# Seven-for-eight block products over three quarters of a feed-forward's depth, remainders by accumulating DMAs, and a down projection in two passes

## The chip, the cores and the metric

One core of a Trainium2 chip runs one launch of the kernel. The metric is the device time of that launch in microseconds (us), as the median of several runs. The engines that appear below are TensorE (PE; its weight loads are shown apart as PEld), VectorE (DVE), ScalarE (ACT), GpSimd (POOL) and SyncE (SP). SP and POOL are used here mainly as queues that issue DMAs; ACT issues a few.

## The reference, cut to what matters

The reference is one layer of a diffusion backbone over 256 latent tokens and 256 context tokens of width 2048: a half-step feed-forward, a mixing of tokens (attention and a long convolution), and a second half-step feed-forward. The change is in the first feed-forward, which runs over both streams:

```
def swiglu(h, w_up, w_down):
    gate, up = jnp.split(h @ w_up, 2, axis=-1)
    return (jax.nn.silu(gate) * up) @ w_down

def half_ffn(s, m, slot, g, w_up, w_down):
    h = modulate(rms_norm(s, g), chunk(m, 3 * slot), chunk(m, 3 * slot + 1))
    return s + 0.5 * chunk(m, 3 * slot + 2) * swiglu(h, w_up, w_down)
```

`w_up` is 2048 x 11264, `w_down` is 5632 x 2048, all in fp32. The vectors `m` (shift, scale, gate) come from a linear map of the conditioning, called adaLN below: nine chunks of 2048, of which two are made at the start and seven while the first feed-forward runs.

## The kernel before, in words

**Precision.** Each fp32 operand is split into a rounded part (hi) and a remainder (lo = value - hi), and a product is three matmuls: hi x hi, hi x lo and lo x hi (`mm3`, L238 to L241). For a weight, ACT makes hi by a copy and DVE makes lo by a subtraction (`weight`, L221 to L235, and `split_to`, L207 to L210).

**Up.** The hidden width is cut into 44 tiles j of 128 gate and 128 up columns. Tiles 0 to 2 (WAVE) are done first, together with the making of the normed input; tiles 3 to 43 run in the loop at the end of the first feed-forward, one after another, through `up` (L425). The input has 16 k-tiles of 128 rows; each is a pair of buffers (hi, lo) of 128 x (2 streams x 256 tokens). A tile j takes four pieces kq of four k-tiles each, and each piece is one weight load of 512 KB (128 x 1024) from SP's queue.

A plain piece is eight products (gate or up, times four k-tiles) with 512 columns, so 24 matmuls 512 wide. A block-product piece treats two k-tiles by (gate, up) and two streams as a 2 x 2 by 2 x 2 block matrix product and does it with seven products of half the width in place of eight (a Strassen-Winograd scheme): for two pairs of k-tiles, 14 products with 256 columns, so 42 matmuls 256 wide. It needs sums of activations, made once by `combine` (L377) for each pair of k-tiles on DVE and ACT; sums of weights, made for each piece on DVE in place (L405 to L407); and a final combination of four banks in `up` (L444 to L450). `prepare` (L397) makes the weights of a piece in two halves, of three and of four blocks of 128 columns; `products` (L412) lists its products. `QUADS = {3: 4, 2: 5}` says that piece 3 is a block product from tile 4 on and piece 2 from tile 5 on. Pieces 0 and 1 are plain in all tiles. The sums are made at the head of tiles 4 and 5, in one go.

The result of a tile goes through SiLU and a product, is split by `keep` (L455) into hi (ACT) and lo (DVE), and both go to DRAM (`act`) by POOL's queue, 256 KB each.

**Down.** `w_down` is cut into 11 groups g of four hidden tiles and eight pairs dq of two output tiles; a step (`step`, L470) is one weight load of 512 KB and 24 matmuls 512 wide. `down` (L486) runs passes: three output pairs, three, then two, and in each pass all 11 groups. For each group `fetch` (L460) brings four tiles x (hi, lo) back from DRAM, eight DMAs of 256 KB on POOL's queue, up to three uses ahead; at most ROOM = 5 groups are held, so a pass can begin with those that the pass before ended with. In the middle of a pass the residual input is loaded. The last APART = 3 groups of the last pass are done by stream, context first and then latent, in matmuls 256 wide, so that the norm of the context can be made beside the latent half (`NORM_PLAN` says how much of it behind each output tile).

**adaLN.** 224 blocks of 512 KB are loaded on SP's queue, each behind the last weight load, and reduced on DVE (L145), once or, for chunks that both streams use, twice. `hook` is called behind each piece of `up` and ahead of each step of `down`; `ada_hook` then does as many blocks as `ADA_RATES` says for one call (2.0 in tiles 4 and 5, then 0.7, and 1.27 in down).

**Order.** A planner places the instructions of each engine: it takes them in program order where their inputs and buffers are ready in its own model of time. Once placed, each engine and each DMA queue works strictly in order. Buffers are shared by tag: "u" has 58 of 2 KB a partition (activations, sums, fetched tiles, temporaries), "raw" four and "whi" and "wlo" three each for weights. PSUM has eight banks, in two tags "pa" and "pb" of four; tile j uses one tag, tile j + 1 the other.

## Time and profile before

| | |
|---|---|
| time, median of 3 runs | 2681.13 us (2680.35 to 2682.34) |
| the profiled execution's own time | 2687.43 us |
| its span on the core | 2685.6 us |
| mean granted clock of TensorE | 0.989 |
| up, tiles 3 to 43 | about 158 to 1038 us |
| down | about 1038 to 1567 us |
| busy in the span: PE, DVE, ACT, POOL | 2625.9, 1897.1, 1018.8, 165.5 us |
| DMA moved | 586.29 MB, mean 218 GB/s |

The profile is of one execution. "Busy" of an engine is the union of its instructions' times; matmuls overlap in the records, so a busy PE may still be slowed. A wait is put down to the instruction that released it last. "PEclk" is the clock granted to TensorE as a share of the full one. Line numbers (L241) are those of the kernel's text above.

### The profile page before, as it was taken

The numbers are of one execution on the slowest core, as the hardware profiler recorded it, in microseconds if no ns is written. First come the engines' busy times: TensorE is split into PE (matmuls) and PEld (weight loads), VectorE is DVE, ScalarE is ACT, GpSimd is POOL, SyncE is SP. The second block draws the span as 40 slices with busy tenths as digits, with TensorE's granted clock in tenths as the row PEclk, the third lists the DMA queues.
The fourth block names the chain that finished last, engine by engine and source line by source line (L and its number), as shares of the span: only waits on it lengthen the run. The fifth ranks groups of instructions, "written<-read, shape, count | busy, mean of one in ns | idle before, by whom it ended". The sixth has DMA issues, their size and how long they took to land.

```text
span 2685.6 us, 36384 instructions
## 1 busy us (share of the span) xinstructions
PE 2625.9 (98%) x13856; PEld 2219.3 (83%) x13856; DVE 1897.1 (71%) x2985; ACT 1018.8 (38%) x1339; POOL 165.5 (6%) x316
## 2 busy tenths in 40 slices
PE   8999999999999998999999999999999999999999
PEld 5677999999999996778777888888888888888887
DVE  5788878877787876678778497789765555554444
ACT  5343333333333332112112265457454444444333
POOL 1100000000000002410101100000000000000000
PEclk8999999999999998999999999999999999999999
DMA  9975555555555559987978855435545655556664
GB/s 357 359 264 182 202 204 196 197 184 193 205 203 192 191 190 330 393 288 242 306 256 276 288 172 184 145 110 160 201 157 190 190 190 189 189 189 206 201 202 158
DMA packets 182476, 586.29 MB, mean 218 GB/s; under 512 B 21020, under 2 KB 24029, under 8 KB 177949
## 3 DMA queue, kind: packets, MB, share of 16 engines
q1 hardware_dynamic: 139580, 500.20, 54.7%
q0 software_dynamic: 41952, 80.50, 9.7%
q10 hardware_dynamic: 768, 3.28, 0.3%
q8 instruction: 108, 1.77, 0.3%
q14 instruction: 68, 0.55, 0.1%
HBM read 556.61 MB, written 27.28 MB: 217 GB/s over the span
## 4 chain that ended last, share of the span: by engine, by line
PE 77%; DMA 10%; DVE 9%; issue 3%; ACT 1%; SPq 0%; DVEq 0%; ACTq 0%
PE pa L1216 10%; PE pa L1217 10%; PE pa L1215 10%; DMA adaw<-in_w_adaT_dram 8%; PE pb L241 6%; PE pa L239 6%; PE pb L239 6%; PE pa L240 6%; PE pb L240 6%; PE pa L241 6%; PE pa L247 3%; DVE adas L145 3%; DVE wlo L232 2%; PE pa L249 2%; PE pb L182 1%
## 5 line engine op out<-in xcount | busy, mean ns | idle before, releaser
L232 DVE TENSOR_TENSOR wlo<-raw,whi 128x1024 fp32r<-128x1024 f32 x558 | 681.5, 1223 | 436.4 <-ACT whi L228 434.8
L228 ACT CAST whi<-raw 128x1024 fp32r<-128x1024 f32 x558 | 586.6, 1052 | 953.8 <-PE pa L1217 413.4
L241 PE MATMUL pa<-u,wlo 128*128 128x512 f32 (+1 forms) x1338 | 461.9, 345 | 6.5 <-DVE wlo L232 6.4
L239 PE MATMUL pa<-u,whi 128*128 128x512 f32 (+1 forms) x1338 | 463.8, 347 | 4.3 <-DMA u<-act 2.2
L240 PE MATMUL pa<-u,whi 128*128 128x512 f32 (+1 forms) x1338 | 462.2, 346 | 5.1 <-DMA u<-act 4.7
L241 PE MATMUL pb<-u,wlo 128*128 128x512 f32 (+1 forms) x1296 | 445.4, 344 | 18.4 <-DVE wlo L232 9.6
L239 PE MATMUL pb<-u,whi 128*128 128x512 f32 (+1 forms) x1296 | 445.3, 344 | 4.4 <-ACT whi L208 3.5
L240 PE MATMUL pb<-u,whi 128*128 128x512 f32 (+1 forms) x1296 | 443.7, 343 | 1.2 <-DVE u L209 1.2
L1215 PE MATMUL pa<-whi,u 128*128 128x512 f32 x1060 | 413.9, 391 | 0.0
L1216 PE MATMUL pa<-wlo,u 128*128 128x512 f32 x1060 | 412.8, 390 | 0.2 <-DVE wlo L232 0.2
L1217 PE MATMUL pa<-whi,u 128*128 128x512 f32 x1060 | 412.8, 390 | 0.0
L241 PEld LDWEIGHTS pb<-u,wlo 128*128 128x128 f32 x1296 | 249.0, 193 | 51.2 <-DVE wlo L232 18.6
L239 PEld LDWEIGHTS pa<-u,whi 128*128 128x128 f32 x1338 | 255.4, 191 | 41.5 <-issue 4.5
L241 PEld LDWEIGHTS pa<-u,wlo 128*128 128x128 f32 x1338 | 255.7, 191 | 38.4 <-DVE wlo L232 8.5
L240 PEld LDWEIGHTS pa<-u,whi 128*128 128x128 f32 x1338 | 255.5, 191 | 36.7 <-DMA u<-act 6.4
L239 PEld LDWEIGHTS pb<-u,whi 128*128 128x128 f32 x1296 | 248.7, 192 | 33.8 <-ACT whi L208 3.9
L240 PEld LDWEIGHTS pb<-u,whi 128*128 128x128 f32 x1296 | 248.9, 192 | 29.2 <-DVE u L209 1.5
L145 DVE CUSTOM_DVE_ANT_0 adas<-adaw,crow,mod 128x1024 bf16<-128x1024 f32 x160 | 205.3, 1283 | 68.1 <-DMA adaw<-in_w_adaT_dram 65.5
L145 DVE CUSTOM_DVE_ANT_0 adas<-adaw,crow,cond 128x1024 bf16<-128x1024 f32 x160 | 205.1, 1282 | 58.4 <-DMA adaw<-in_w_adaT_dram 56.4
L208 ACT CAST whi<-raw 128x768 fp32r<-128x768 f32 (+1 forms) x158 | 148.8, 943 | 245.3 <-DVE raw L407 169.7
L209 DVE TENSOR_TENSOR wlo<-raw,whi 128x768 fp32r<-128x768 f32 (+1 forms) x158 | 171.7, 1089 | 89.8 <-ACT whi L208 87.3
L1216 PEld LDWEIGHTS pa<-wlo,u 128*128 128x128 f32 x1060 | 199.1, 188 | 41.5 <-DVE wlo L232 0.6
(326 smaller groups left out, 2817.0 us busy)
## 6 DMA issues: line engine op xcount, KB each, us to landing
adaw<-in_w_adaT_dram SPq DMA_DIRECT2D x222, 512.0 KB, 5.8
raw<-in_w_dn_dram SPq DMA_DIRECT2D x182, 512.0 KB, 4.3
raw<-in_w_up_dram SPq DMA_DIRECT2D x176, 512.0 KB, 3.5
raw<-in_w_up1q_dram SPq DMA_DIRECT2D x164, 512.0 KB, 3.9
u<-act POOLq DMA_DIRECT2D x184, 256.0 KB, 8.0
wrow<-in_w_ada_dram SPq DMA_DIRECT2D x32, 1024.0 KB, 9.1
act<-u POOLq DMA_DIRECT2D x88, 256.0 KB, 2.3
raw<-in_w_hy_dram SPq DMA_DIRECT2D x32, 512.0 KB, 3.5
```

Of the source, the lines that this page charges most:

```text
L145: V.tensor_tensor_reduce(out=sc, in0=t, in1=crow[i][:, b * (D // 2) : (b + 1) * (D // 2)], scale=1.0, scalar=mcol if b else bada[:, n : n ...
L208: S.copy(hi, src)
L209: V.tensor_sub(lo, src, hi.bitcast(F32))
L228: S.copy(hi, raw)
L232: V.tensor_sub(lo, raw, hi.bitcast(F32))
L239: PE.matmul(ps, w[0], xx[0], start=start, stop=False)
L240: PE.matmul(ps, w[0], xx[1], start=False, stop=False)
L241: return PE.matmul(ps, w[1], xx[0], start=False, stop=stop)
L247: PE.matmul(ps, w[0], x, start=start, stop=stop)
L1215: PE.matmul(ps[t], hi, w[0], start=start, stop=False)
L1216: PE.matmul(ps[t], hi, w[1], start=False, stop=False)
L1217: last = PE.matmul(ps[t], lo, w[0], start=False, stop=stop)
```

## The change

It has four parts.

1. Block products for three of the four pieces: piece 3 from tile 5, piece 2 from tile 7, piece 1 from tile 9. `combine` becomes a generator of four parts for each pair of k-tiles; one part is run by the hook behind each piece, from tile 3 on, and one sum, which overwrites part of a plain operand, is put in place at the end of the tile before its first use (`install`).
2. Piece 0 stays plain, but its weights are made without DVE: ACT writes hi and then -hi, and a DMA on POOL's queue adds the raw weights to it in SBUF, 256 KB for each of two halves. Its buffers come from "u".
3. `keep` does the same for the activation's remainder, in DRAM: hi and -hi are stored, then the value is added by a third DMA to what the second has stored.
4. Down runs in two passes of four output pairs, eight banks each; the last two groups (APART = 2) are done by stream, with two output tiles to a bank. The adaLN rates become 0.79 for each piece of up from tile 4 on and 1.25 for each step of down.

```diff
 WAVE = 3
 ADA_UP = (5, 7, 6, 8)
 ADA_DOWN = (2, 3, 4)
-ADA_RATES = (2.0, 0.7, 1.27)
-QUADS = {3: 4, 2: 5}
+ADA_RATES = (0.79, 1.25)
+QUADS = {3: 5, 2: 7, 1: 9}
 GT = JT // GRP
-PASSES = ((0, 1, 2), (3, 4, 5), (6, 7))
-ORDERS = ((9, 8, 10, 7, 6, 5, 4, 3, 2, 1, 0), tuple(range(GT)), tuple(reversed(range(GT))))
+PASSES = ((0, 1, 2, 3), (4, 5, 6, 7))
+ORDERS = ((9, 8, 10, 7, 6, 5, 4, 3, 2, 1, 0), tuple(range(GT)))
 ROOM = 5
-APART = 3
-NORM_PLAN = (0, 1, 0, 1, 0, 1, 1, 1, 1, 1, 1, 1)
+APART = 2
+NORM_PLAN = (0, 1, 0, 1, 0, 1, 1, 1, 1, 1, 1, 1, 1, 1, 1, 1)
 
 AWAKE = (17, 5)
 
...
             self.h = [None] * KT
             self.mm = mm3
             self.held = {}
-            self.sums = {}
+            self.sums, self.first = {}, {}
             self.wupq = a["w_up1q"]
 
         def open(self, alt=False):
...
             return mm
 
         def close(self, j, ps2):
-            sg = tmp2((P, 2, L))
+            sg = U((P, 2, L))
             S.activation(sg, ps2[0], AF.Silu)
             V.tensor_mul(sg, ps2[1], sg)
             self.keep(j, sg)
...
         def combine(self, kp):
 
             (h0, l0), (h1, l1) = self.h[2 * kp], self.h[2 * kp + 1]
-            a0, a1, b0, b1 = tmp((P, 2, L)), tmp((P, 2, L)), tmp2((P, 2, L)), tmp2((P, 2, L))
+            a0, a1, b0, b1 = (U((P, 2, L)) for _ in range(4))
             V.tensor_add(a0, h0.bitcast(F32), l0.bitcast(F32))
             V.tensor_add(a1, h1.bitcast(F32), l1.bitcast(F32))
+            yield
             V.tensor_add(b0[:, 0, :], a0[:, 1, :], a1[:, 1, :])
             V.tensor_sub(b1[:, 0, :], b0[:, 0, :], a0[:, 0, :])
+            yield
             V.tensor_sub(b1[:, 1, :], a0[:, 1, :], a0[:, 0, :])
             V.tensor_sub(b0[:, 1, :], a1[:, 0, :], b1[:, 0, :])
+            yield
             s23, s4 = split(b1, (P, 2, L)), U((P, 2, L), F32R)
-            split_to(b0[:, 0, :], h0[:, 1, :], l0[:, 1, :])
             split_to(b0[:, 1, :], s4[:, 0, :], s4[:, 1, :])
             self.sums[kp] = [(h0[:, 0, :], l0[:, 0, :]), (h1[:, 0, :], l1[:, 0, :]), (s4[:, 0, :], s4[:, 1, :]),
                              (h1[:, 1, :], l1[:, 1, :]), (h0[:, 1, :], l0[:, 1, :]),
                              tuple(t[:, 0, :] for t in s23), tuple(t[:, 1, :] for t in s23)]
+            self.first[kp] = b0[:, 0, :]
+            yield
+
+        def build(self):
+            for kq in QUADS:
+                for kp in (2 * kq, 2 * kq + 1):
+                    yield from self.combine(kp)
+
+        def install(self, kq):
+            for kp in (2 * kq, 2 * kq + 1):
+                split_to(self.first.pop(kp), *self.sums[kp][4])
 
         def quads(self, j, kq):
             return j >= QUADS.get(kq, JT)
 
         def prepare(self, j, kq):
 
-            if not self.quads(j, kq):
-                return [weight(self.wupq[j - WAVE, kq], (P, 2, 4, P))]
             raw = weight_load(self.wupq[j - WAVE, kq], (P, 2, 4, P))
             out = []
+            if kq == 0:
+                hi, lo = ([U((P, 4, P), F32R) for _ in range(2)] for _ in range(2))
+                for q in range(2):
+                    S.copy(hi[q], raw[:, q])
+                    S.activation(lo[q], hi[q].bitcast(F32), AF.Copy, scale=-1.0)
+                    nc.gpsimd.dma_start(lo[q], raw[:, q].bitcast(F32R), accum_op=ALU.add)
+                return [(hi, lo)]
+            if not self.quads(j, kq):
+                return [weight(None, (P, 2, 4, P), raw=raw)]
             for n in (3, 4):
                 if n == 4:
                     V.tensor_sub(raw[:, :, 0:4:3], raw[:, :, 3:4].broadcast_to((P, 2, 2, P)), raw[:, :, 0:3:2])
...
                     ps = banks[bank] if part is None else banks[bank][:, part, :]
                     xx = self.h[x] if part is None else self.sums[x[0]][x[1]]
                     left[bank] -= 1
-                    mm3(ps, [t[:, q, block] for t in w[n]], xx, left[bank] == total[bank] - 1, left[bank] == 0)
+                    mm3(ps, [t[q][:, block] if kq == 0 else t[:, q, block] for t in w[n]], xx, left[bank] == total[bank] - 1, left[bank] == 0)
                 w = None
                 if j == JT - 1 and kq == 1:
                     self.fetch(ORDERS[0][0])
                 self.hook()
+            for kq in QUADS:
+                if QUADS[kq] == j + 1:
+                    self.install(kq)
             if not total[2]:
                 return self.close(j, banks)
-            g, v, u = tmp((P, 2, L)), tmp2((P, 2, L)), T(up, (P, L), "mt", bufs=3)
+            g, v, u = tmp((P, 2, L)), U((P, 2, L)), T(up, (P, L), "mt", bufs=3)
             S.copy(g[:, 0, :], banks[2][:, 0, :])
             V.tensor_add(u, g[:, 0, :], banks[2][:, 1, :])
             V.tensor_add(g[:, 1, :], u, banks[3][:, 0, :])
...
             self.keep(j, v)
 
         def keep(self, j, act):
-            act = split(act, (P, 2, L))
-            for s_ in range(2):
-                nc.gpsimd.dma_start(actd[j][:, s_], act[s_])
+
+            hi, minus = U((P, 2, L), F32R), U((P, 2, L), F32R)
+            S.copy(hi, act)
+            S.activation(minus, hi.bitcast(F32), AF.Copy, scale=-1.0)
+            nc.gpsimd.dma_start(actd[j][:, 0], hi)
+            nc.gpsimd.dma_start(actd[j][:, 1], minus)
+            nc.gpsimd.dma_start(actd[j][:, 1], act.bitcast(F32R), accum_op=ALU.add)
 
         def fetch(self, g):
 
...
                         nc.gpsimd.dma_start(act[s_], actd[j][:, s_])
                     self.held[g].append(act)
 
-        def step(self, g, dq, banks, begin, end, parts=None, done_=None):
+        def step(self, g, dq, banks, begin, end, part=None, done_=None):
 
             whi, wlo = weight(self.wdown[g, dq], (P, GRP, 2, P))
             for i2 in range(2):
                 d = dq * 2 + i2
                 for jj, act in enumerate(self.held[g]):
-                    ps = banks[d]
-                    act = act if parts is None else [t[:, parts, :] for t in act]
-                    self.mm(ps, (whi[:, jj, i2, :], wlo[:, jj, i2, :]), act, begin and jj == 0, end and jj == GRP - 1)
-                if end:
-                    for i in range(2) if parts is None else (parts,):
-                        V.scalar_tensor_tensor(xd(i, d), ps[:, i, :] if parts is None else ps, mod[i][self.cm + 2][:, d : d + 1], xd(i, d),
-                                               op0=ALU.mult, op1=ALU.add)
+                    ps = banks[d] if part is None else banks[dq][:, i2, :]
+                    act = act if part is None else [t[:, part, :] for t in act]
+                    self.mm(ps, (whi[:, jj, i2, :], wlo[:, jj, i2, :]), act, begin and jj == 0 and not (i2 and part is not None),
+                            end and jj == GRP - 1 and (i2 == 1 or part is None))
+                if end and part is None:
+                    for i in range(2):
+                        self.add(i, d, ps[:, i, :])
                 if done_:
                     done_()
+            if end and part is not None:
+                for i2 in range(2):
+                    self.add(part, dq * 2 + i2, banks[dq][:, i2, :])
+
+        def add(self, i, d, ps):
+            V.scalar_tensor_tensor(xd(i, d), ps, mod[i][self.cm + 2][:, d : d + 1], xd(i, d), op0=ALU.mult, op1=ALU.add)
 
         def down(self, after):
 
             uses = [(p, g) for p in range(len(PASSES)) for g in ORDERS[p]]
             for n, (p, g) in enumerate(uses):
                 if g == ORDERS[p][0]:
-                    tags = (PA, PA, PA, PA, PB, PB) if p == 0 else (PB, PB, PA, PA, PA, PA) if p == 1 else (PB,) * 4
-                    banks = {2 * dq + i2: tags[2 * k + i2]((P, 2, L)) for k, dq in enumerate(PASSES[p]) for i2 in range(2)}
+                    banks = {2 * dq + i2: (PA, PB)[k // 2]((P, 2, L)) for k, dq in enumerate(PASSES[p]) for i2 in range(2)}
                 for _, soon in uses[n : n + 3]:
                     self.fetch(soon)
                     while len(self.held) > ROOM:
...
             yield
             rest = [g for _, g in uses[-APART:]]
             for part in (1, 0):
-                banks = {d: (PA if part else PB)((P, L)) for d in range(2 * PASSES[-1][0], KT)}
+                banks = {dq: (PA if part else PB)((P, 2, L)) for dq in PASSES[-1]}
                 for g in rest:
                     self.fetch(g)
                     for dq in PASSES[-1]:
...
     crow = []
 
     xs = [[None] * (KT // 2) for _ in range(2)]
-    ready = {j: kq for kq, j in QUADS.items()}
+    build = f1.build()
+    f1.hook = lambda: next(build, None)
+    rate[0] = ADA_RATES[0]
     for j in range(WAVE, JT):
-        if j in ready:
-            for kp in (2 * ready[j], 2 * ready[j] + 1):
-                f1.combine(kp)
         f1.up(j, ahead if j == WAVE else None)
-        rate[0] = ADA_RATES[j >= 5]
         if j == WAVE:
             for i in range(2):
                 crow.append(T(adap, (P, D), f"crow{i}", bufs=1))
                 nc.scalar.dma_start(crow[i], a["crow"][i : i + 1, :].partition_broadcast(P))
                 S.activation(crow[i], crow[i], AF.Silu)
-            f1.hook = ada_hook
+            f1.hook = lambda: (next(build, None), ada_hook())
     rs1 = U((P, 2, L))
     cont, lat = [], []
 
...
 
     more = mix_input(1, cont, PASSES[-1][0], PA)
     norm_plan = iter(NORM_PLAN)
-    rate[0] = ADA_RATES[2]
+    f1.hook, rate[0] = ada_hook, ADA_RATES[1]
     downs = f1.down(lambda: [next(more) for _ in range(next(norm_plan))])
     next(downs)
     while done[0] < len(todo):
```

## The prediction

> **What bounds the kernel now.** I read the page first, then a table of the stages that the change touches.
>
> ```profile
> span 2685.6 us, 36384 instructions
> ...
> PE 2625.9 (98%) x13856; PEld 2219.3 (83%) x13856; DVE 1897.1 (71%) x2985; ACT 1018.8 (38%) x1339; POOL 165.5 (6%) x316
> ```
>
> ```profile
> core 0: us, PE busy (x) PEld busy (x) DVE busy (x) ACT busy (x) POOL busy (x), PEclk, DMA share, GB/s
> ...
> 158.20:201.40 43.20, 43.20 (x212) 36.60 (x211) 36.09 (x62) 19.44 (x25) 5.35 (x10) 1.00 0.88 304
> 201.40:233.80 32.40, 25.96 (x135) 22.20 (x134) 30.72 (x54) 9.65 (x16) 1.07 (x2) 0.89 0.51 183
> 233.80:1010.40 776.60, 776.60 (x4887) 706.30 (x4886) 619.89 (x974) 273.38 (x334) 39.45 (x74) 1.00 0.57 196
> 1010.40:1037.60 27.20, 23.04 (x134) 20.94 (x133) 20.45 (x35) 7.39 (x10) 5.31 (x10) 0.90 0.88 287
> 1037.60:1243.20 205.60, 191.68 (x795) 154.29 (x794) 153.76 (x248) 36.45 (x37) 49.82 (x94) 0.94 0.95 323
> 1243.20:1435.30 192.10, 184.35 (x794) 149.91 (x793) 150.96 (x232) 36.34 (x36) 22.25 (x42) 0.98 0.79 268
> 1435.30:1528.80 93.50, 88.42 (x385) 71.69 (x384) 59.70 (x102) 17.89 (x19) 22.24 (x42) 1.00 0.97 324
> 1528.80:1567.00 38.20, 37.40 (x309) 36.88 (x307) 26.89 (x46) 23.35 (x34) 0.00 (x0) 1.00 0.47 149
> ```
>
> The stages are, in order: up tiles 3 and 4; tile 5; tiles 6 to 42; tile 43; down passes 0, 1 and 2; the two halves by stream. TensorE (PE) is never idle in tiles 6 to 42, so there only less matmul time helps. A busy PE does not tell what one matmul costs; the spacing of starts in the timeline does. Below stand two 512-wide matmuls six places apart, then two 256-wide ones 69 places apart.
>
> ```profile
> 599.78 0.39 PE L241 MATMUL pb<-u,wlo 128*128 128x512 f32 x1
> ...
> 601.14 0.39 PE L241 MATMUL pb<-u,wlo 128*128 128x512 f32 x1
> 601.37 0.28 PE L239 MATMUL pb<-u,whi 128*128 128x256 f32 x1
> ...
> 609.64 0.28 PE L239 MATMUL pb<-u,whi 128*128 128x256 f32 x1
> ```
>
> 1.36/6 = 0.2267 us and 8.27/69 = 0.1199 us. A plain piece (24 wide matmuls) costs 5.44 us, a block-product piece (42 narrow ones) 5.04. Two of each make a tile of 20.95 us, and 37 tiles 775 us: the 776.6 of the third row. So the other stages lose: tile 5, 32.4 - 20.95 = 11.4; tile 43, 6.2; pass 0, 205.6 - 33 x 5.44 = 26.0; pass 1, 12.5; pass 2, 93.5 - 16 x 5.44 = 6.4; the halves, 38.2 - 288 x 0.1199 = 3.7. The down stage loses 48.6 in all.
>
> **Up: matmul time.** Before, 40 + 39 = 79 pieces are block products; after, tiles from 5, 7 and 9 on give 39 + 37 + 35 = 111. 32 more, each 5.44 - 5.04 = 0.405 us cheaper, all on PE's unbroken path: **-13.0 us**. The steady tile becomes 5.44 + 3 x 5.04 = 20.55 us. The Trainium skill (TensorE: Matmul & The Clock Gate, Back-to-back issue gap) gives a gap of N/2.4 + 2.5 ns: 216 and 109 ns, by which a piece would save 0.59 us and the term be -19. The trace disagrees by 11 ns at both widths (227 and 120), and the sum goes by the trace.
>
> **Up: the combining of activations.** Tile 5's loss is `combine`, run in one burst ahead of the tile:
>
> ```profile
> ACT whi L208 <- DVE raw L407: 11.2, 2, 9.0
> ...
> PEld pb L239 <- ACT whi L208: 3.9, 2, 2.9
> ```
>
> VectorE (DVE) is 30.7 of 32.4 us busy there, ScalarE (ACT) waits 9.0 us once for its differences, and PE waits for ACT. The burst ahead of tile 4 cost nothing (first row, PE busy throughout). The change cuts each k-tile pair's work into four parts, one behind each piece, so that the six pairs are spread over tiles 3 to 8 and the last sums of each quarter are made three, two and one pieces before their first use. I take 2 us left of 11.4: **-9.4** (bounds 0 and -11.4). The buffers keep it from all of it: tag "u" has 58, of which 32 hold activations and 18 the sums; with the last pair's four temporaries and the four now taken by a kq = 0 piece there are none to spare in tiles 7 and 8.
>
> **Up: the work on the other engines.** Durations from the steady stage (300 to 1000 us; L407 equals L406):
>
> ```profile
> L209 DVE TENSOR_TENSOR wlo<-raw,whi 128x1024 fp32r<-128x1024 f32 x67 | 82.0, 1224 | 54.1 <-ACT whi L208 51.7 <-PE pa L240 1.2 <-PE pb L241 1.2
> L232 DVE TENSOR_TENSOR wlo<-raw,whi 128x1024 fp32r<-128x1024 f32 x66 | 80.3, 1223 | 14.9 <-ACT whi L228 14.3
> L209 DVE TENSOR_TENSOR wlo<-raw,whi 128x768 fp32r<-128x768 f32 x67 | 64.0, 955 | 26.6 <-ACT whi L208 26.6
> L145 DVE CUSTOM_DVE_ANT_0 adas<-adaw,crow,mod 128x1024 bf16<-128x1024 f32 x47 | 60.2, 1281 | 10.6 <-DMA adaw<-in_w_adaT_dram 10.4
> L405 DVE TENSOR_TENSOR raw<-raw 128x512 f32<-128x512 f32 x67 | 46.1, 688 | 1.1
> L406 DVE TENSOR_TENSOR raw<-raw 128x256 f32<-128x256 f32 x67 | 28.2, 421 | 1.1
> L204 DVE TENSOR_TENSOR u<-sg,u 128x512 fp32r<-128x512 f32 x34 | 23.3, 686 | 0.0
> ```
>
> ```profile
> L208 ACT CAST whi<-raw 128x1024 fp32r<-128x1024 f32 x67 | 70.3, 1050 | 160.1 <-DVE raw L407 135.1 <-DVE mod L154 13.4 <-DVE mod L156 11.6
> ...
> L203 ACT CAST u<-sg 128x512 fp32r<-128x512 f32 x34 | 21.2, 622 | 37.4 <-DVE sg L452 37.4
> ```
>
> ```profile
> L458 POOL DMA_DIRECT2D act<-u x68 | 36.3, 533 | 677.6 <-ACT u L203 640.0 <-DVE u L204 34.0 <-DVE wlo L209 3.5
> ```
>
> DVE per tile: kq = 1 turns 1.22 into 0.69 + 2 x 0.42 + 0.96 + 1.22 = 3.71; kq = 0 drops 1.22; the activation's remainder drops 0.69; the rate 0.79 for 0.7 adds 0.36 adaLN blocks, 0.46. Sum +1.04 on 619.89/37 = 16.75, so 17.8 of 20.55 us, 87% for 80%. That still fits. What it hits first is the chain behind three block-product pieces in a row: a piece's second half has its three differences, then ACT's copy (1.05), then DVE's remainder (1.22), and its buffer (three of each) comes free two half-pieces, 5.04 us, before it is needed. Copy and remainder take 2.3, which leaves 2.7 us for whatever else DVE has queued: two adaLN blocks (2.6) use it up. Before, two plain pieces followed and refilled the lead; now it is kq = 0, which needs no such buffer, 5.44 us. I allow 0.1 us a tile: **+4** (bounds 0 and one block of 1.3 us on 35 tiles, +45).
>
> kq = 0 now needs four ACT passes of 0.62 and two accumulating DMAs of 256 KB from GpSimd's (POOL's) queue. No run shows such a DMA. The nearest rows bound its landing: a plain store from the same queue in this stage, and a fetch while the DMA engines were full.
>
> ```profile
> act<-u POOLq DMA_DIRECT2D x68, 256.0 KB, 2.3
> ```
>
> ```profile
> u<-act POOLq DMA_DIRECT2D x92, 256.0 KB, 9.6
> adaw<-in_w_adaT_dram SPq DMA_DIRECT2D x40, 512.0 KB, 7.8
> raw<-in_w_dn_dram SPq DMA_DIRECT2D x32, 512.0 KB, 5.3
> ```
>
> When ACT makes them is set by the planner's order. In the trace the next tile's plain copies stand ahead of the close of the tile before:
>
> ```profile
> 606.52 1.05 ACT L228 CAST whi<-raw 128x1024 fp32r<-128x1024 f32 x1 [0.56 <-PE pb L240]
> ...
> 611.28 0.37 ACT L444 COPY sq<-pb 128x256 f32<-128x256 f32 x1 [1.54 <-PE pb L241]
> ```
>
> If that holds, the buffers of the current kq = 0 piece come free 5.44 us into a tile and 15.1 are left. Four passes (2.5), two issues (1.1) and one landing of 2.3 to 9.6 make 5.9 to 13.2: hidden, **0**. I take it nearer 2.3, since the engines are at 57% in this stage. `keep` now has three DMAs, and the third waits in POOL's queue for the second to land, some 2.3 us, with the next tile's two remainders or, after tile 43, the fetch of group 8 queued behind it. The first lies inside the same slack; the second is counted below. Extra bytes (0.79 MB a tile for the three accumulating DMAs' sources, 0.19 for adaLN, on 196 GB/s) give some 248 GB/s.
>
> **Down.** Steps: 82 of 5.44 plus 288 narrow matmuls (480.6 us) become 80 plus 384 (481.2): **+0.6**; the two more weight loads and splits lie under PE. Lost time is what moves. In pass 0 the engines are full (0.95), and this is what PE ends up waiting for over the whole stage, and DVE from 1006 to 1500 us:
>
> ```profile
> PE pb L241 <- DVE wlo L232: 9.3, 7, 2.2
> PE pa L241 <- DVE wlo L232: 6.4, 3, 4.2
> PE pa L240 <- DMA u<-act: 4.7, 4, 1.5
> PE pb L241 <- DVE mod L156: 4.0, 1, 4.0
> ```
>
> ```profile
> DVE adas L145 <- DMA adaw<-in_w_adaT_dram: 95.5, 44, 8.7
> ```
>
> A late adaLN block holds DVE, DVE holds the weight remainder, PE stops, and the granted clock falls (0.94 in pass 0). The fetch of activations crowds the queues. It falls from 184 DMAs,
>
> ```profile
> u<-act POOLq DMA_DIRECT2D x184, 256.0 KB, 8.0
> ```
>
> or 23 groups of eight, to 22 - 5 held = 17 groups: 48 DMAs or 12.6 MB less. Per group, pass 0 moves 2.1 + 3 x (0.52 + 1.27 x 0.52) = 5.7 MB in 16.3 us (347 GB/s); after, 2.1 + 4 x (0.52 + 1.25 x 0.52) = 6.8 MB in 21.8 us (313). Pass 2's losses go with its pass. The start stays bad: groups 8 and 10 can only be fetched once tile 43's stores are out, 2.2 us later than now (0.62 - 0.69 + 2.3), against 5.4 us more cover from group 9's fourth step. I put what is left at 17 in pass 0, 8 in pass 1, 3 in the halves, 28 for 48.6: **-20.6** (bounds 0 and, a third of it left, -32). PSUM: pass 0 now takes all eight banks, and its third step needs those that tile 43 holds; it comes 10.9 us after that tile's last matmul, and the close reads them in its first six steps, some 3 us (4 x 0.42 + 2 x 0.69). Tile 43's 6.2 stay.
>
> **Sum:** -13.0 - 9.4 + 4 + 0.6 - 20.6 = -38.4. The profiled execution took 2687.4 us (span 2685.6), 6.3 above the median; from 2687.4 that is 2649, from the median of 2681.1 it is **2642.7**.
>
> **Rivals.** *Late remainders* (slower): the accumulating DMA adds a second read per element, and a pair stands behind one another in the same queue. If a pair lands 17.4 - 3.6 = 13.8 us after issue, 1.4 times the crowded 9.6, PE waits 17.4 - 15.1 = 2.3 us in 41 tiles, +94: 2737. It decides from 0.94 us per tile on. For it: nothing shows this operation. Against: 2.3 us landings at 57% load. The Trainium skill (SBUF — State Buffer, Who interferes with whom) warns that GpSimd's descriptors starve while VectorE holds their shared port in its two-port modes; by that rule more DMAs on this queue would be late. The trace does not show it: 533 ns an issue with VectorE 80% busy. Chance 0.08. *The chain binds*: 1 us for each of 35 tiles, +35 in place of +4: 2674 to 2679, no change; for it 2.7 us of lead, against it that the same chain cost nothing in tiles 6 to 42. 0.08. *The passes bring nothing*: adaLN and weights alone keep the blocks late: 2663, 0.08; pass 1 lost 12.5 at a share of 0.79. *All waits go*: down loses 12, combining and chain nothing: -13.0 - 11.4 + 0.6 - 36.6 = -60.4, 2621; for it the middle of pass 1, at low load; 0.16.
>
> **Numbers.** The forecast holds 0.60, its own range 2625 to 2660. 2612 to 2676 leaves out the slower case, half of the no-change case and tails. Faster by over 0.2% (5.4 us, about what a measurement here can tell): 0.60 + 0.16 + 0.08 = 0.84; same 0.08; slower 0.08.
>
> **What would show it.** Tiles 9 to 42 at 20.55 us with PE busy throughout; no gap near tile 5; landing of `u<-raw` under 9.6 us; 136 fetches; DVE's wait for `adaw` well below 95.5. The prediction is wrong if PE waits for `u<-raw` at tile starts, if DVE's L209 shows as PE's releaser in the steady stage, or if the two passes still lose over 45 us.

## The result and the profile after

| | before (same chip) | after |
|---|---|---|
| time, median of 4 runs each | 2681.74 us (2680.35 to 2683.43) | 3180.99 us (3176.80 to 3183.79) |
| ratio, 95% interval | | 1.186 (1.184 to 1.188) |
| span of the profiled execution | 2685.6 us (an earlier run) | 3182.0 us |

Slower by 499 us where 38 us less was forecast. The page after:

```profile
span 3182.0 us, 38107 instructions
...
PE 2752.6 (87%) x14480; PEld 2334.4 (73%) x14480; DVE 1914.0 (60%) x3050; ACT 1124.6 (35%) x1545; POOL 254.2 (8%) x394
...
PEclk9998788888887887787999999999999999999999
```

PE fell from 98% to 87% busy and DVE from 71% to 60%: no engine has become the bound, all wait. PEclk shows where: slices 4 to 19, which is the up stage. Windows of one steady up tile, of down's full passes and of the halves by stream (columns as in the prediction):

```profile
422.33:456.49 34.16, 24.77 (x151) 22.47 (x151) 17.56 (x29) 9.97 (x15) 3.77 (x6) 0.80 0.52 146
1534.28:2006.28 472.00, 444.92 (x1921) 362.16 (x1920) 353.56 (x561) 88.46 (x89) 69.84 (x131) 0.98 0.83 284
2006.28:2055.10 48.82, 48.82 (x405) 48.53 (x403) 36.21 (x62) 28.41 (x41) 0.00 (x0) 1.00 0.50 151
```

This tile takes 34.2 us and not 20.55, 13.6 more. Tiles 3 to 42 all take between 31 and 35.1 us, and tiles 3 to 43 together some 1380 for the 879 of before: that is the whole difference. Down with its halves took 520.8 us for 529.4 before. PE's timeline at the head of that tile (the bracket is the idle time before, and its releaser):

```profile
422.33 0.79 PE L239 MATMUL pb<-u,u 128*128 128x512 f32 x1 [8.64 <-ACT u L417]
...
423.35 0.63 PE L239 MATMUL pb<-u,u 128*128 128x512 f32 x1
423.78 0.63 PE L240 MATMUL pb<-u,u 128*128 128x512 f32 x1
...
426.65 1.22 PE L241 MATMUL pb<-u,u 128*128 128x512 f32 x2 [0.75 <-DMA u<-raw]
...
430.65 0.60 PE L240 MATMUL pb<-u,u 128*128 128x512 f32 x1
...
432.03 0.39 PE L239 MATMUL pb<-u,u 128*128 128x512 f32 x1
432.25 0.39 PE L240 MATMUL pb<-u,u 128*128 128x512 f32 x1
```

PE stands 8.64 us, waiting for ScalarE's first copy of piece 0 (L417). Then two 512-wide matmuls start 0.43 us apart, about twice the 0.227 of before, and only after some 8.5 us 0.22 us apart again. The granted clock was 0.50 in those 8.5 us (last section). Waiting for the remainder by the adding DMA adds 0.75 us. So 8.64 and 0.75 us idle make 9.4 of the 13.6, and the rest, some 4.2 us, goes to the half clock. ScalarE at the next head:

```profile
453.17 0.63 ACT L474 ACTIVATE sq<-sq 128x512 f32<-128x512 f32 x1 [3.74 <-DVE sq L472]
454.65 0.62 ACT L481 CAST u<-u 128x512 fp32r<-128x512 f32 x1 [0.84 <-DVE u L475]
455.30 0.63 ACT L482 ACTIVATE u<-u 128x512 fp32r<-128x512 f32 x1
455.83 0.60 ACT L417 CAST u<-raw 128x512 fp32r<-128x512 f32 x1
456.47 0.63 ACT L418 ACTIVATE u<-u 128x512 fp32r<-128x512 f32 x1
```

Piece 0 of the new tile (L417, L418) stands directly behind the close of the old one: SiLU (L474), then the two passes of `keep` (L481, L482), which wait for VectorE's sums. In the profile before, the next tile's copies stood ahead of the close. The waits of 400 to 1300 us (engine, line, what for: us in total, times, longest) and the adding DMA's row (count, size, median us to landing):

```profile
PEld pb L239 <- ACT u L417: 119.6, 13, 11.2
...
PEld pa L239 <- ACT u L417: 111.6, 13, 9.2
...
PE pa L241 <- DMA u<-raw: 13.6, 13, 2.0
```

```profile
u<-raw POOLq DMA_DIRECT2D x82, 256.0 KB, 4.0
```

231 us in 26 tiles is 8.9 a tile for the copy, and 1 us a tile for the DMA, which lands in 4.0 us.

### The profile page after: what moved, and what is told of

Its sections match the earlier page's. It is cut to its first block, busy times and chain, and to the rows that moved or that the text cites. A ratio compares the mean times of both kernels' runs of the same rounds, so it can differ in the third digit from the quotient of the medians.

```text
span 3182.0 us, 38107 instructions
## 1 busy us (share of the span) xinstructions
PE 2752.6 (87%) x14480; PEld 2334.4 (73%) x14480; DVE 1914.0 (60%) x3050; ACT 1124.6 (35%) x1545; POOL 254.2 (8%) x394
## 3 DMA queue, kind: packets, MB, share of 16 engines
q0 software_dynamic: 53184, 100.95, 13.6%
## 4 chain that ended last, share of the span: by engine, by line
PE 40%; issue 40%; DMA 9%; DVE 6%; POOL 4%; ACT 1%; SPq 0%; POOLq 0%; DVEq 0%; ACTq 0%
PE pa L1246 8%; PE pa L1247 8%; PE pa L1245 8%; DMA adaw<-in_w_adaT_dram 6%; PE pa L247 3%; DVE adas L145 3%; DVE wlo L232 2%; PE pa L249 1%; PE pb L241 1%; PE pb L239 1%; PE pb L240 1%; POOL act L485 1%; POOL u L419 1%; PE pa L239 1%; PE pa L241 1%
## 5 line engine op out<-in xcount | busy, mean ns | idle before, releaser
L232 DVE TENSOR_TENSOR wlo<-raw,whi 128x1024 fp32r<-128x1024 f32 x487 | 595.4, 1223 | 435.5 <-ACT whi L228 433.7
L228 ACT CAST whi<-raw 128x1024 fp32r<-128x1024 f32 x487 | 512.2, 1052 | 923.6 <-PE pa L1247 413.4
L208 ACT CAST whi<-raw 128x768 fp32r<-128x768 f32 x222 | 208.5, 940 | 723.0 <-PE pb L240 253.9
L241 PE MATMUL pb<-u,wlo 128*128 128x256 f32 (+1 forms) x1262 | 405.6, 322 | 19.2 <-DVE wlo L232 11.2
L239 PE MATMUL pa<-u,whi 128*128 128x256 f32 (+1 forms) x1252 | 411.8, 330 | 4.7 <-DMA u<-act 2.6
L240 PE MATMUL pa<-u,whi 128*128 128x256 f32 (+1 forms) x1252 | 407.1, 326 | 7.0 <-DMA u<-act 6.6
L239 PE MATMUL pb<-u,whi 128*128 128x256 f32 (+1 forms) x1262 | 409.4, 324 | 2.0 <-ACT whi L208 2.0
L241 PE MATMUL pa<-u,wlo 128*128 128x256 f32 (+1 forms) x1252 | 405.9, 325 | 0.0
L240 PE MATMUL pb<-u,whi 128*128 128x256 f32 (+1 forms) x1262 | 404.6, 321 | 0.0
L209 DVE TENSOR_TENSOR wlo<-raw,whi 128x768 fp32r<-128x768 f32 x222 | 241.5, 1090 | 228.8 <-ACT whi L208 228.0
L145 DVE CUSTOM_DVE_ANT_0 adas<-adaw,crow,mod 128x1024 bf16<-128x1024 f32 x160 | 205.3, 1283 | 245.1 <-DMA adaw<-in_w_adaT_dram 242.6
L145 DVE CUSTOM_DVE_ANT_0 adas<-adaw,crow,cond 128x1024 bf16<-128x1024 f32 x160 | 205.1, 1282 | 225.9 <-DMA adaw<-in_w_adaT_dram 224.0
L239 PEld LDWEIGHTS pa<-u,whi 128*128 128x128 f32 x1252 | 246.4, 197 | 32.5 <-issue 5.3
L240 PEld LDWEIGHTS pa<-u,whi 128*128 128x128 f32 x1252 | 244.7, 195 | 28.2 <-DMA u<-act 8.1
L239 PE MATMUL pb<-u,u 128*128 128x512 f32 (+1 forms) x232 | 111.0, 481 | 168.9 <-ACT u L417 168.9
```

The lines of the kernel that those rows point to most:

```text
L145: V.tensor_tensor_reduce(out=sc, in0=t, in1=crow[i][:, b * (D // 2) : (b + 1) * (D // 2)], scale=1.0, scalar=mcol if b else bada[:, n : n ...
L208: S.copy(hi, src)
L209: V.tensor_sub(lo, src, hi.bitcast(F32))
L228: S.copy(hi, raw)
L232: V.tensor_sub(lo, raw, hi.bitcast(F32))
L239: PE.matmul(ps, w[0], xx[0], start=start, stop=False)
```

## The experiments

The time of each is a median, and each ratio is to the kernel before on the same chip (2681.6 to 2684.6 us).

| run | what it is | us | ratio, 95% interval |
|---|---|---|---|
| e1 | change, piece 0 ahead of the close | 2821.4 | 1.052 (1.049 to 1.054) |
| e2 | change, piece 0 in a tag of its own | 2786.8 | 1.040 (1.037 to 1.042) |
| e3 | change, piece 0's remainders by VectorE | 2691.6 | 1.004 (1.003 to 1.006) |
| e4 | before, with the two passes alone | 2669.9 | 0.995 (0.994 to 0.997) |
| e5 | e1, adaLN loads behind an earlier load | 2817.0 | 1.051 (1.049 to 1.052) |
| e6 | e1 without the up stage's adaLN blocks | 2666.6 (1 run) | |
| e7 | e4 and the spread combining, half the range | 2666.4 | 0.994 (0.992 to 0.996) |
| e8 | e3, no adding DMA at all | 2700.3 | 1.007 (1.006 to 1.009) |
| e9 | e1, adaLN loads two blocks ahead | 2823.2 | 1.052 (1.051 to 1.054) |
| e10 | e1, one adaLN load for all blocks | 2707.2 (1 run) | |
| e11 | e9, no adding DMA in tiles 3, 4 and 43's activation | 2808.8 | 1.047 (1.045 to 1.049) |
| e12 | e7, adaLN loads two blocks ahead | 2670.6 | 0.995 (0.993 to 0.997) |
| e13 | e1, adaLN loads on ScalarE's queue | 2949.7 | 1.099 (1.098 to 1.101) |
| e14 | e1, five raw buffers | 2821.4 | 1.052 (1.050 to 1.053) |
| e15 | e13 with e11's edges | 2936.0 | 1.093 (1.091 to 1.095) |
| e16 | e7, adaLN loads on ScalarE's queue | 2708.4 | 1.009 (1.008 to 1.011) |
| e17 | e9, each block pinned behind its own piece | 2662.7 | 0.993 (0.991 to 0.995) |
| e18 | e17 with e11's edges | 2641.9 | 0.986 (0.984 to 0.987) |

### The first cause: e1, e2 and e3

Theory A: the planner hands out the buffers of a tag in program order. Piece 0's four tiles now come from tag "u", as do the close's `v`, `hi` and `minus`, which stand ahead of them in the program; before, they came from "whi" and "wlo". Rival B: "u" is simply short. Rival C: the adding DMA is slow. e1 changes the program order alone:

```diff
+            self.ready = [self.prepare(j + 1, 0)] if j + 1 < JT else [None]
             if not total[2]:
                 return self.close(j, banks)
...
-        f1.up(j, ahead if j == WAVE else None)
+        f1.up(j, ahead if j == WAVE else f1.ready[0])
```

> The changed kernel with one thing moved: the next tile's piece 0 (its load, ACT's four passes and the two adding DMAs) is written into the program ahead of the close of the current tile; the number of buffers and of instructions stays. Theory A (order): the four buffers of piece 0 come from the same tag as the close's three, a tag's buffers are handed out in program order, so the copies had to stand on ACT behind the close. Then the idle time of some 8.6 us at the head of each tile goes, tiles 9 to 42 take 20.6 us, and the time is 2640 to 2670 us. Theory B (shortage): the tag has too few free buffers (58, of which 50 are held), whatever the order; then the tiles stay above 30 us and the time above 3000. Theory C (slow adding DMA): PE waits for the adding DMA; then the tiles stay above 25 us.

e2 leaves the order and takes the tag away:

```diff
-                hi, lo = ([U((P, 4, P), F32R) for _ in range(2)] for _ in range(2))
+                hi, lo = ([T(up, (P, 4, P), "k0", F32R, 4) for _ in range(2)] for _ in range(2))
...
-        return T(up, shape, "u", dt, 58)
+        return T(up, shape, "u", dt, 54)
-    ROOM = 5
+    ROOM = 4
```

> The changed kernel with the four buffers of piece 0 in a tag of their own; the other tag has 54 in place of 58 and down holds 4 groups in place of 5, so that it fetches one more. The program order stays. Theory A (order within the tag): the copies can now go ahead of the close, tiles take 20.6 us, and the time is 2640 to 2690 us, some of it lost in down to the extra fetch. Theory B (shortage): four buffers for the piece and 4 fewer for the rest make it no better: above 3000. A third reading, that the planner puts the copies late because of its own times and not because of the tag, also expects above 3000.

e3 makes piece 0 by `weight`, with VectorE's subtraction:

```diff
             if kq == 0:
-                hi, lo = ([U((P, 4, P), F32R) for _ in range(2)] for _ in range(2))
-                for q in range(2):
-                    S.copy(hi[q], raw[:, q])
-                    S.activation(lo[q], hi[q].bitcast(F32), AF.Copy, scale=-1.0)
-                    nc.gpsimd.dma_start(lo[q], raw[:, q].bitcast(F32R), accum_op=ALU.add)
-                return [(hi, lo)]
+                hi, lo = weight(None, (P, 2, 4, P), raw=raw)
+                return [([hi[:, q] for q in range(2)], [lo[:, q] for q in range(2)])]
```

> The changed kernel with the remainder of piece 0 made by VectorE in the weights' own buffers as before; the other parts stay (three quarters as block products, activations' remainders by the adding DMA, two passes). Theories A, B and C all expect the loss to go. What it tells is whether VectorE can carry it: its work per tile is 17.8 + 1.2 = 19 us of 20.55, so I expect some waits for its remainders, tiles of 21 to 23 us and a time of 2660 to 2740 us. If it comes out at or under 2650, the relief of VectorE by the adding DMA was not needed.

Measured: 2821.4, 2786.8 and 2691.6 us, all far under 3181. In e1 and e2 PE never waits for L417 again between 400 and 1100 us. That shows A: with four tiles fewer in "u", e2 has no more room than the change, and the wait still goes; so B falls, and C with it, since e1 and e2 keep the adding DMAs. But neither comes near the forecast. The tiles of e1 take 20.6 to 29.9 us in no steady pattern, and PE now waits for VectorE's remainder (L209). PE's two largest waits in e1 between 400 and 1100 us:

```profile
PE pb L241 <- DVE wlo L209: 26.5, 21, 2.5
PE pa L241 <- DVE wlo L209: 21.3, 14, 4.4
```

The two causes do not add up: the second was there in the change too (VectorE waits 147 us for adaw between 500 and 1000 us, for 15 in the kernel before), covered by the first.

### The second cause: e5, e6, e9, e10, e13, e14, e17

SyncE's queue in e1, then VectorE at the same time:

```profile
625.35 0.33 SPq L216 DMA_DIRECT2D raw<-in_w_up1q_dram  x1
625.72 0.43 SPq L141 DMA_DIRECT2D adaw<-in_w_adaT_dram  x1
626.19 7.40 SPq L216 DMA_DIRECT2D raw<-in_w_up1q_dram  x2
633.64 0.44 SPq L141 DMA_DIRECT2D adaw<-in_w_adaT_dram  x1
```

```profile
624.99 0.42 DVE L427 TENSOR_TENSOR raw<-raw 128x256 f32<-128x256 f32 x1
630.81 1.28 DVE L145 CUSTOM_DVE_ANT_0 adas<-adaw,crow,mod 128x1024 bf16<-128x1024 f32 x1 [5.40 <-DMA adaw<-in_w_adaT_dram]
...
632.02 1.22 DVE L209 TENSOR_TENSOR wlo<-raw,whi 128x1024 fp32r<-128x1024 f32 x1
```

VectorE stands 5.40 us at an adaLN block (L145) whose load was issued 5.09 us before the reading began, that is 0.3 us after VectorE had come to it. The weight remainder that PE needs (L209) is next in VectorE's queue. On SyncE's queue the next block's load stood behind two weight loads. Their row merges two short issues, of 0.43 and 0.33 us, and the 6.6 us between them in which SyncE waited for a raw buffer. Theory D: the loads are late because of SyncE's queue. The first attempt orders it behind an earlier weight load:

```diff
-            with tc.issue_after(last_load[0].ins):
+            with tc.issue_after(loads[-3].ins):
                 nc.sync.dma_start(t, src)
```

> As e1_before_close, but each adaLN block's load (adaw) is ordered behind the third last weight load issued, no longer behind the last. Theory D: what is left in e1 (tiles of some 24.9 us for 20.55) is a loop: adaw stands on SyncE's queue behind a weight load that waits for a raw buffer, VectorE waits for adaw (98 us in 500 to 1000), and the raw buffer comes free only by VectorE's remainder. Then the wait of L145 for adaw falls below 30 us, the tiles come to 21 to 22 us, and the time to 2690 to 2720 us. Rival E (VectorE and ScalarE are simply too late behind three block products in a row, the prediction's chain): the tiles stay above 24 us and the time at 2800 to 2840 us, with or without the wait for adaw.

2817.0 us, no difference, and adaw still waited for 97 us. The time from a load's issue to its reduction did not grow (median 6.2 us for 6.7 in e1, 450 to 950 us), so e5 tells nothing. e6 takes the blocks out:

```diff
         def ada_next():
...
-            ada_dve(c, d, b)
+            if c in ADA_DOWN:
+                ada_dve(c, d, b)
```

> As e1_before_close, but the adaLN blocks that run beside the up stage are left out: their data isn't loaded and not reduced, and constants stand in for their results. Theory D: without adaw there is no loop; VectorE also has some 2 us a tile less to do; tiles at 20.5 to 21.0 us, 2650 to 2690 us in all. Rival E: the chain behind three block products stays, tiles above 23 us, over 2760 us.

2666.6 us. From tile 9 on every tile but the last takes 20.6 us. So three block products in a row run at the forecast pace, and the blocks are the second cause, by their loads or by their 1.28 us each. e10 keeps VectorE's work and drops the loads; e9 keeps both and loads two blocks earlier:

```diff
+        if c in ADA_UP and same:
+            t = same[0]
+        else:
+            t = T(adap, (P, D // 2), "adaw", bufs=4)
...
+        if c in ADA_UP:
+            same[:] = [t]
```

> As e1_before_close, but the adaLN blocks of the up stage all reduce the first block's data, which is loaded once: the loads are left out, VectorE's work is all there. Theory D: nothing to wait for, tiles at 20.6 to 21 us, 2655 to 2690 us. Rival F: tiles above 23 us, above 2750 us.

```diff
+            for k in range(done[0], min(done[0] + 1 + LEAD, len(todo))):
+                if k not in early:
+                    early[k] = ada_load(*todo[k])
             c, d, b = todo[done[0]]
-            ada_dve(c, d, b)
+            ada_dve(c, d, b, early[done[0]])
```

> As e1_before_close (2821.4 us), but each adaLN block's load is issued two blocks before the block that reads it, into the same four buffers; VectorE's work is unchanged. In e6 the up stage ran at 20.58 us a tile without the blocks. Theory D (the load of adaw comes too late, since SyncE's queue stands behind a weight load that waits for its buffer): VectorE no longer waits for adaw, the tiles come to 20.6 to 21 us, and the time to 2660 to 2690 us. Rival F (it is the 1.28 us of each block on VectorE, ahead of the remainders): the wait for adaw goes, the tiles stay above 23 us, and the time is above 2750 us.

e10 gave 2707.2 us: from 540 us on 20.6 us a tile, but 25 us a tile from 332 to 540 us. It is a miss by its number (2655 to 2690), and it doesn't separate D from F. With no load to wait for, the planner moved the reductions ahead: 74 of them lie between 332 and 540 us, some nine a tile, and none between 540 and 1038 us. So the fast tiles are tiles without blocks, as in e6, and in the slow ones VectorE is busy 198.77 of 208 us (columns as in the prediction):

```profile
332.00:540.00 208.00, 182.24 (x1223) 167.13 (x1222) 198.77 (x349) 80.04 (x114) 30.99 (x42) 0.96 0.55 136
```

e9 gave 2823.2 us, nothing. Its trace says why: from the issue of a block's load to the start of its reduction (pairing loads and reductions in order, 450 to 950 us, medians) it is 6.7 us in e1 and 6.6 in e9. The planner had moved the reduction forward with the load. e13 and e14 try the queue and the buffers:

```diff
-                nc.sync.dma_start(t, src)
+                (nc.scalar if act else nc.sync).dma_start(t, src)
```

> As e1_before_close (2821.4 us), but in the up stage the adaLN blocks are loaded from ScalarE's queue, each behind the last weight copy there, and no longer from SyncE's behind the last weight load. Same bytes, same work on VectorE. Theory D' (SyncE's queue is blocked by a weight load that waits for the raw buffer which piece 0 holds until its adding DMAs have landed, and adaw with it): tiles of 20.6 to 21.5 us, the wait for adaw under 30 us in 500 to 1000, 2660 to 2700 us. Rival G (the loads' traffic slows the adding DMAs and the weights): tiles stay above 23 us, over 2760 us.

```diff
-        raw = T(wp, shape, "raw", bufs=4)
+        raw = T(wp, shape, "raw", bufs=5)
```

> As e1_before_close, but five raw buffers for four (tag u has 56 tiles for 58). By theory D' one buffer more covers the one that piece 0 holds: SyncE waits less, tiles of 20.6 to 22 us, 2660 to 2720 us. If the traffic is the cause (rival G), no change: 2790 to 2840 us.

Both miss: 2949.7 us, worse by 128, and 2821.4, the same. The lead was 4.7 us in e13 (the load stands behind ScalarE's copy of the same piece, the reduction right behind that piece's remainder) and 6.8 in e14. VectorE's waits for adaw between 500 and 1000 us in e1, e9, e14, e13 and, for comparison, e3:

```profile
DVE adas L145 <- DMA adaw<-in_w_adaT_dram: 98.4, 33, 7.5
```

```profile
DVE adas L149 <- DMA adaw<-in_w_adaT_dram: 95.5, 31, 8.0
```

```profile
DVE adas L145 <- DMA adaw<-in_w_adaT_dram: 83.2, 29, 6.0
```

```profile
DVE adas L147 <- DMA adaw<-in_w_adaT_dram: 70.6, 46, 4.5
```

```profile
DVE adas L145 <- DMA adaw<-in_w_adaT_dram: 10.8, 12, 2.2
```

This lead runs to the start of the reduction, so it contains the wait itself, and its median hides the spread. Between 500 and 1000 us VectorE came to 13 of e1's 62 blocks less than 2 us after their load's issue, to two of them before it, and these 13 make 61 of its 99 us of waiting. In the kernel before it came to no block earlier than 3.7 us after the issue.

None of these runs lengthened the lead, so none of them tests theory D as it was meant; in e14 SyncE still waited 182 us for raw buffers that adding DMAs read (177 in e1). Theory H looks at the other end of the gap: what counts is where the reduction stands in VectorE's order. e17 is e9 with the reduction ordered behind the remainder that is last in the program there:

```diff
+        last_lo[:] = [V.tensor_sub(lo, src, hi.bitcast(F32))]
...
+            with ExitStack() as order:
+              if c in ADA_UP and last_lo:
+                order.enter_context(tc.issue_after(last_lo[0].ins))
+              V.tensor_tensor_reduce(
```

> As e9_ahead_prefetch (2823.2 us), and on VectorE each adaLN block of the up stage is ordered behind the weight remainder that is last in the program at that place, so that it can't move forward with its earlier load: in VectorE's order the blocks stand some six remainders later than in e9. Theory H (VectorE stands at a block whose data has not landed, 95 us in 500 to 1000, and the differences and remainders of the weights wait behind it): the wait for adaw falls below 15 us, the tiles come to 20.6 to 21.2 us, the time to 2660 to 2700 us. Rival G (the loads' traffic): tiles above 23 us, over 2760 us. Rival F' (1.28 us of a block right behind a remainder delays the next piece's differences): the wait goes and the tiles stay at 21.5 to 23 us, 2700 to 2760 us.

2662.7 us, within the 2660 to 2700 expected. The lead is now 25.4 us in the median and 16.4 at the least, and adaw is no longer among VectorE's waits. The window 500 to 1000 us in e1 and e17 (sum, then PE, PEld, DVE, ACT, POOL, clock, DMA share, GB/s):

```profile
500.00:1000.00 500.00, 437.61 (x2963) 409.09 (x2962) 352.16 (x576) 193.20 (x280) 75.56 (x100) 0.95 0.70 202
```

```profile
500.00:1000.00 500.00, 499.88 (x3637) 475.86 (x3636) 428.83 (x710) 234.88 (x338) 91.10 (x121) 1.00 0.85 246
```

In e17 PE does 3637 matmuls for 2963 and is never idle, with VectorE busier (429 for 352 us) and the DMA engines too (0.85 for 0.70). That rules out traffic (G) and VectorE's load (F, F') as causes: e17 has more of both, with 76 blocks for 62, and loses nothing there. SyncE still waits 150 us for buffers that adding DMAs read, and each load stands at about the same place among the weight loads as in e9. So it is the place of the reading that mends it. Whether ordering the reading would do without the two blocks of earlier loading was not run.

### Parts of the change by themselves: e4, e7, e8, and variants

e4 puts only part 4's passes on the kernel before (with `step` and `down` as in the change):

```diff
-PASSES = ((0, 1, 2), (3, 4, 5), (6, 7))
+PASSES = ((0, 1, 2, 3), (4, 5, 6, 7))
...
-APART = 3
+APART = 2
```

> The kernel before with the two passes of down alone (eight banks, last two groups by stream); up as before, rates as before. My prediction's term for the passes was -20.6 us, so 2661. The changed kernel's down stage, read from the trace, took 524 us against 529, which would give about 2676. No theory of the loss in up bears on it.

2669.9 us, 9 above the 2661 of the prediction's term. Its down stage with the halves took 511.9 us for 529.4:

```profile
1034.80:1497.80 463.00, 446.19 (x1922) 364.20 (x1922) 361.29 (x576) 87.59 (x87) 68.89 (x130) 0.98 0.85 291
1497.80:1546.70 48.90, 48.90 (x405) 48.56 (x403) 36.48 (x63) 28.48 (x41) 0.00 (x0) 1.00 0.51 162
```

463.0 less 80 steps of 5.44 is 27.8 us lost, and the halves lose 2.8: 30.6, where 28 was forecast. e7 adds the spread combining for half the range, with rates of 0.76 and 1.27:

```diff
-QUADS = {3: 4, 2: 5}
+QUADS = {3: 5, 2: 7}
...
+    build = f1.build()
+    f1.hook = lambda: next(build, None)
```

> As e4_passes_alone (2669.9 us), with the combining of the activations spread over the pieces of tiles 3 to 6 as the change has it, for half of the k-range only, and the block products from tile 5 (quarter 3) and 7 (quarter 2) on. Prediction's step: the burst at tile 5 loses 11.4 us and the spread leaves 2; two block-product pieces become plain for two and one tiles more (3 x 2 pieces... by the table 1 + 2 pieces, 0.4 us each, +1.2). So 2669.9 - 9.4 + 1.2 = 2661.7 us. Rival: the loss moves to tiles 6 to 8 (buffers of tag u) and the time stays within 3 us of 2670.

2666.4 us. The up stage ended 8.7 us earlier than in e4 (1026.1 for 1034.8), as expected. Behind it most was lost again: the passes took 2.7 us more, the stages behind the halves 4.9, and the medians differ by 3.5 us. e8 has no adding DMA; it is e3 with `keep` as before:

```diff
-            hi, minus = U((P, 2, L), F32R), U((P, 2, L), F32R)
...
-            nc.gpsimd.dma_start(actd[j][:, 1], act.bitcast(F32R), accum_op=ALU.add)
+            act = split(act, (P, 2, L))
+            for s_ in range(2):
+                nc.gpsimd.dma_start(actd[j][:, s_], act[s_])
```

> As e3_piece0_vector (2691.6 us: the change with piece 0's remainders made by VectorE), and the activation's remainder made by VectorE too, so that no adding DMA is left. If keep's three DMAs are what delays the start of the down stage (12 us longer than in e4's 463 us), the down stage falls to some 463 us and the time to 2680 us. If not, VectorE has 0.69 us a tile more to do, the tiles grow by up to that, and the time is 2692 to 2715 us.

2700.3 us, 9 more than e3: the 0.69 us a tile on VectorE costs more than `keep`'s third DMA. The full passes of its down stage took 472 us (476 in e3), so the third DMA explains at most 4 of the 13 us by which e3's are longer than e4's. e12 and e16 carry e9's and e13's edits to e7 and fail like them:

> As e7_passes_and_spread (2666.4 us), with the loads of the adaLN blocks two blocks ahead as in e9. In the down stage of e7 VectorE still waits for adaw and PE for VectorE's remainders; of some 29 us that the passes lose I expect 5 to 12 us back: 2655 to 2662 us. If the passes lose by the full DMA queues alone, 2664 to 2668 us.

> As e7_passes_and_spread (2666.4 us), with the up stage's adaLN loads from ScalarE's queue. The up stage of e7 has no stall to gain from; 2662 to 2668 us by either theory.

e12: 2670.6 us, no gain. e16: 2708.4 us, 42 worse than e7; my "no stall to gain from" overlooked that the edit can make one.

### The edges: e11, e15, e18

Tiles 3 and 4 come directly behind the wave. In e17 PE waits there for the adding DMA (155 to 217 us):

```profile
PE pa L249 <- DMA u<-raw: 8.8, 1, 8.8
PE pb L249 <- DMA u<-raw: 3.4, 1, 3.4
```

In tile 3 (the 3.4 us) the first DMA was issued 0.5 us after the tile began and took 6.2 us to land. In tile 4 (the 8.8) ScalarE was done with both halves at 183.5 us, before the tile began, but POOL issued their DMAs only from 189.2 on:

```profile
176.78 0.92 POOL L493 DMA_DIRECT2D act<-u  x1
188.67 0.86 POOL L494 DMA_DIRECT2D act<-u  x1 [10.97 <-DVE u L390]
189.23 2.10 POOL L427 DMA_DIRECT2D u<-raw  x2
```

Ahead of them stood `keep`'s third DMA for tile 2 (L494), which waits for the second (L493) to land. That took from 176.8 to 188.2 us; the VectorE instruction that the row names had ended long before.

The mended edges make these two by VectorE, and tile 43's activation as well:

```diff
+                if j < WAVE + 2:
+                    hi, lo = weight(None, (P, 2, 4, P), raw=raw)
+                    return [([hi[:, q] for q in range(2)], [lo[:, q] for q in range(2)])]
...
+            if j == JT - 1:
+                for s_, t in enumerate(split(act, (P, 2, L))):
+                    nc.gpsimd.dma_start(actd[j][:, s_], t)
+                return
```

> As e9_ahead_prefetch, and piece 0 of the first two tiles (3 and 4) and the last tile's activation have their remainders made by VectorE, no adding DMA. In e6 PE waited 5.5 us for the adding DMA in those two tiles and then ran at half clock for some us, and the down stage's start waited for the last tile's third store. Theory D: 2645 to 2665 us, below e4 (2669.9) and e7 (2666.4); rival F: above 2730 us.

> As e13_ada_own_queue, and piece 0 of tiles 3 and 4 and the activation of the last tile made without adding DMAs (as e11_all_mended, without its earlier loads). By theory D' some 10 us below e13: 2648 to 2680 us, the whole change near its forecast of 2643. By rival G over 2750 us.

> As e17_reduce_pinned (2662.7 us), and piece 0 of tiles 3 and 4 and the last tile's activation have their remainders made by VectorE, no adding DMA. In e6 PE waited 5.5 us for those DMAs in the two tiles and ran at half clock for some 6 us more; the third store of the last tile delays the fetch of group 8. If both go: 2645 to 2655 us. If the start is bounded by something else: 2658 to 2666 us.

e11 (2808.8) and e15 (2936.0) rest on e9 and e13 and keep their losses, 14 us below each. e18 rests on e17: 2641.9 us, 20.8 below it, 0.986 of the kernel before (0.984 to 0.987), the fastest of all. Its page, and windows of tiles 3 to 8, 9 to 42, 43, the passes and the halves:

```profile
span 2637.0 us, 38215 instructions
...
PE 2599.2 (99%) x14480; PEld 2230.2 (85%) x14480; DVE 1911.9 (73%) x3053; ACT 1113.3 (42%) x1538; POOL 248.7 (9%) x389
```

```profile
155.01:284.66 129.65, 128.76 (x687) 111.42 (x686) 96.14 (x163) 62.62 (x93) 25.82 (x36) 1.00 0.84 247
284.66:987.19 702.53, 701.96 (x5103) 668.04 (x5101) 601.99 (x989) 330.59 (x477) 127.89 (x170) 1.00 0.85 245
987.19:1007.84 20.65, 20.65 (x152) 19.67 (x151) 17.54 (x31) 8.78 (x12) 6.27 (x11) 1.00 0.99 303
1007.84:1464.27 456.43, 442.28 (x1923) 361.73 (x1921) 362.89 (x579) 87.71 (x88) 68.69 (x130) 0.99 0.85 296
1464.27:1513.20 48.93, 48.93 (x405) 48.59 (x403) 36.32 (x62) 28.50 (x41) 0.00 (x0) 1.00 0.49 151
```

## Why the prediction was wrong

Its sign was wrong because of two steps, both about order and not about work. e17 mends these two. e18 also takes the adding DMA out of tiles 3 and 4 and of tile 43's activation, and its stages check the rest of the sum.

- **Piece 0 hidden, 0 us: the step that failed.** The text had "When ACT makes them is set by the planner's order. In the trace the next tile's plain copies stand ahead of the close of the tile before", and went on from "if that holds". The trace showed that order for copies into "whi" and "wlo"; the change writes into "u", where the close allocates first. It did not hold, and 15.1 us of slack became 8.6 us of idle PE, 13.6 a tile with the half clock and the 0.75 us for the adding DMA. e1 and e2 show the cause. The prediction gave the condition no price and no chance.
- **The chain behind three block products, +4 (0 to +45): the second step that failed.** It counted the 1.28 us of a block as VectorE's only cost, and looked for waits on adaw in the down stage alone. What cost e9 160 us against e17 was VectorE standing at a block whose data had not landed. With the order mended, the term comes out: tiles 9 to 42 of e18 take 702.53/34 = 20.66 us for 20.55, so +3.8. That is partly luck, since the 0.1 us a tile was an allowance and not worked out.
- **Late remainders** saw PE waiting at tile starts, but for the wrong thing: the adding DMA landed in 4.0 us (6.4 in e17), under the 9.6 taken as the bound, and PE waited for ScalarE. PE waited long for the DMA itself only in tiles 3 and 4. In tile 4 `keep`'s third DMA held it up in POOL's queue. The prediction had seen that queueing, but put it at some 2.3 us inside the slack; there the second store took 11.4 us to land. Issuing an adding DMA took POOL 0.90 us on average with VectorE 53% busy (the change, 300 to 1000 us) and 0.99 with 86% (e17). The rule that the Trainium skill (SBUF — State Buffer, Who interferes with whom) gives, that GpSimd's descriptors starve while VectorE holds their shared port in its two-port modes, made no difference here that the time shows; no row shows in which mode VectorE ran, so this doesn't test it.
- **Matmul time, -13.0 us:** right. 34 tiles at the 20.99 us of before are 713.7 us, so tiles 9 to 42 took 11.1 less. The sum had 34 x 0.405 = -13.8 there; with the chain's +3.8, and without the 0.04 a tile that they lost before (-1.3), it gives -11.3.
- **Combining, -9.4 us:** right. Tiles 3 to 8 took 43.2 + 32.4 + 3 x 20.99 = 138.6 us before and 129.65 in e18, 8.9 less although three pieces became plain (+1.2): -10.1.
- **VectorE 87% busy:** 601.99/702.53 is 86%. That it "still fits" was right.
- **Down, +0.6 and -20.6 us:** right in size by the profiles: -17.5 in e4 and -24.0 in e18 (529.4 to 505.4). By medians e4 gained 13.0. In the change itself it was -8.6; its full passes took 472.0 us for e4's 463.0, and no run shows more of that than the 4 us of e8. The wait that was to fall, VectorE's for adaw (95.5 us before), came to 81.6 in e4's passes and 59.9 in e18's, so it fell less than "well below" said.
- **Tile 43's 6.2 us "stay":** wrong. In e18 that tile takes 20.65 us, as in e17. It still took 23.7 in e9, which lacks only the order of the reductions, and 26.4 in e6, which lacks the blocks; what freed it was not tried alone.
- **The sum.** e18 against before, by spans: tiles 3 to 43 -26.6, down -24.0, the wave before -3.2, the stages behind +5.2: -48.6 for -38.4. By medians, 2641.9 for 2643. That the two medians meet within 1 us is partly luck: with the two orders alone mended (e17) the time is 2662.7, and tile 43's gain was no term of the sum. So the terms of work were good, and the forecast holds for a kernel that places its instructions as the prediction assumed and makes the remainders at its edges on VectorE, not for the one that was changed.

**Open:** why the planner brings VectorE to some of e1's blocks so soon after their loads, and to none in the kernel before; a late SyncE queue fits e1's rows but wasn't shown to be the reason. Also the 5 us that e7 and e18 lose behind down.
